# Trunk of two hybrid layers: background dosed by an account of VectorE's backlog, block products chained in PSUM, sums of x in larger pieces

## The chip, the cores and the metric

The kernel runs on one core of a Trainium2 chip. The metric is the device time of one execution in microseconds. The kernel before takes 1490.68 us, the median of three runs (1489.7 to 1491.52). TensorE does the matmuls, VectorE and ScalarE the elementwise work, GpSimd a few masks and the transfers that add into memory, and SyncE issues most other transfers. Each engine runs its own queue of instructions in the order of the program and waits by semaphores for the others.

## The reference

Two layers, each with one projection in, two mixers side by side and one projection out, for a sequence of 256 and a model width of 2048, all in float32:

```python
def hybrid_layer(x, ...):
    u = rms_norm(x, norm_g)
    p = u @ w_in                                  # 2048 x 12304
    qk, v, o, z_a, ig, fg, xb, z_b = jnp.split(p, SPLIT_AT, axis=-1)
    qk = jax.nn.silu(causal_dwconv(qk, qk_conv))
    q, k = jnp.split(qk, 2, axis=-1)
    ...
    h = mlstm_chunkwise(q, k, v, i_pre, log_f)    # 8 heads, matrix memory
    h = h * jax.nn.sigmoid(o)
    h = ((h - mu) * lax.rsqrt(var + EPS)) * head_norm_g
    y_a = h * jax.nn.silu(z_a)
    xc = causal_dwconv(xb, lru_conv_w) + lru_conv_b
    y_b = rg_lru(xc, w_a, b_a, w_x, b_x, lam) * jax.nn.silu(z_b)
    return x + jnp.concatenate([y_a, y_b], axis=-1) @ w_out

def reference(x, ...):
    for l in range(DEPTH):                        # DEPTH = 2
        x = hybrid_layer(x, ...)
    return rms_norm(x, final_g)
```

## The kernel before

**Split products.** Every float32 product is three matmuls in the type float32r: a weight piece W is split into a rounded part `wH` (a cast on ScalarE) and a rest `wL` = W - wH (a subtraction on VectorE), and x likewise. A product is then x_H wH + x_H wL + x_L wH.

**Halves.** The work of TensorE is a list of halves, `order_`. A plain half reads a piece of 128 x 1024 weights and makes 12 matmuls of 512 columns. `prepare` (splits) runs `AHEAD` = 3 halves ahead of the matmuls, and there are four buffers for `wH` and four for `wL`. A raw buffer is loaded by SyncE and becomes free when its second split is done; there are three. After the matmuls of a half, its `after` function evacuates the result if an output is complete.

**Groups.** Each layer has four groups g of two heads. For each group come the projections `o`, `qk`, `v`, `xb`, `z`, `zb`, the gates of the recurrent unit and the products with `w_out` (`out`). Results of `qk`, `xb` and others are in token order and are turned into channels by a transposition on VectorE (`blk`), a store (`moved`) and a load (`fr`).

**Background.** What follows a projection (convolutions `qc` and `xc`, the decay matrix `E`, scores, the scan `xc<-a,gate`, the gating `zb`, `ybH`, `ybL`) is written as generators in a list `bg`. After each plain half `pump` steps through them: a generator does a few instructions and yields what they cost in us of VectorE, or the word "wait", which hands the turn to the next generator. `pump(budget)` grants a fixed amount per half: 1.05 us if at most two main generators are in the list, otherwise 2.6; an overdraft is carried on as a negative credit. `require(key)` steps the generators without regard to the credit until something named is done. `V` and `S` are VectorE and ScalarE behind a proxy that orders each of their background instructions after the last split but one or the last cast that has been written (`LAG`).

**Seven products.** Two projections (`z` of group 2, `o` of group 3) are computed together as a 2 x 2 block product with seven block products instead of eight. A block product is four halves of 6 matmuls (`product`, PSUM tile `ps_b`, lines 1145 to 1147), so 28 short halves are strewn between the plain ones of a layer. They need four sums of blocks of x, S1 to S4, made by `block_sums` on VectorE into two buffers `sums` (S3 and S2 in the first, S1 and S4 in the second), in four pieces of 128 x 256 each with five rows (three additions, a cast, a subtraction). They also need sums of weight blocks, made in memory (`w_d`) by transfers that add, in `weight_sums`. The seven results are combined in `res`, four slots of 128 x 512, by copies and additions after each product, and by three more additions in the background (`end6`).

**The end.** In the last layer the last group's `out` is computed with the second half of its rows in weights that are split into buffers of their own, `w_own`.

## Time and profile before

| | |
|---|---|
| profiled execution, own time | 1490.24 us |
| its span, first to last instruction | 1488.5 us |
| granted TensorE clock | 0.999 |
| TensorE matmuls | 6782 |
| ScalarE busy | 954.8 us, 64% |
| bytes moved from and to memory | 274 GB/s over the span |
| chain that ended last | PE 80%, DVE 8%, DMA 6%, issue 4%, ACT 2% |

In the page PE is TensorE's matmul, PEld its load of the stationary operand, DVE VectorE, ACT ScalarE, POOL GpSimd and SP SyncE. A row of the timeline gives start, duration, engine, line, operation, `out<-in`, shapes, a count, and in brackets how long the engine was idle before it and what ended that. Rows of a group give count, busy time, mean duration in ns and idle time before them. Line L112 is the proxy of `V` and `S`, so nearly all rows of VectorE and ScalarE have it, and names of tiles tell them apart.

Matmuls overlap: each is shown with its whole latency, so TensorE's busy time counts small waits as work. The distance from one start to the next tells more.

### The profile page before, as it was taken

The page shows a single profiled execution, that of the slowest core. Times are in us where ns is not written, and L with a number is a line of the kernel's source. Part 1 is how long each engine was busy: PE and PEld are TensorE (multiplying, and loading weights), DVE is VectorE, ACT ScalarE, POOL GpSimd, SP SyncE. Part 2 cuts the span into 40 slices and gives each one's busy share as a digit, 9 for nine tenths or more (in the row PEclk, how much of TensorE's full clock was granted, in tenths as well). Part 3 has the DMA queues.
Part 4 walks back from the last instruction along what each step waited for, and adds up shares of the span by engine and source line. Part 5 has one row for each costly group of instructions (what it writes and reads, how often), then busy time and mean ns, then how long its engine had stood idle before and what let it go on. Part 6 is the DMA issues. An engine that isn't in the chain of part 4 may idle for free.

```text
span 1488.5 us, 18861 instructions
## 1 busy us (share of the span) xinstructions
PE 1473.6 (99%) x6782; PEld 1226.3 (82%) x6782; DVE 1156.6 (78%) x1648; ACT 954.8 (64%) x1226; POOL 112.2 (8%) x186
## 2 busy tenths in 40 slices
PE   9999999999999999999999999999999999999997
PEld 7888888888888888888788887888888888888886
DVE  5788997687887776778867888977888877767775
ACT  7666766567565765658565567665676567655665
POOL 0020010100100000100000100000001000010002
PEclk9999999999999999999999999999999999999999
DMA  9867898898987988886786667778799668777773
GB/s 331 328 203 245 269 338 268 280 268 268 290 291 249 287 287 265 283 272 234 249 302 198 216 203 235 258 233 264 249 269 322 217 222 247 234 238 263 237 269 123
DMA packets 104046, 383.44 MB, mean 258 GB/s; under 512 B 11392, under 2 KB 31888, under 8 KB 84496
## 3 DMA queue, kind: packets, MB, share of 16 engines
q1 hardware_dynamic: 87536, 327.41, 62.8%
q0 software_dynamic: 13952, 50.35, 15.2%
q10 hardware_dynamic: 2464, 4.47, 0.8%
q8 instruction: 53, 0.87, 0.2%
q14 instruction: 41, 0.34, 0.1%
HBM read 344.95 MB, written 62.41 MB: 274 GB/s over the span
## 4 chain that ended last, share of the span: by engine, by line
PE 80%; DVE 8%; DMA 6%; issue 4%; ACT 2%; SPq 0%; POOL 0%; POOLq 0%; ACTq 0%; DVEq 0%
PE acc L395 67%; DVE wL L112 3%; PE ps_gt L840 2%; DMA x_d<-stage 2%; PE ps_b L1147 1%; PE ps_b L1146 1%; PE ps_b L1145 1%; DMA raw<-in_ws_dram 1%; PE acc L408 1%; DMA rawb<-in_ws_dram 1%; DVE xc L112 1%; DVE gate L112 1%; ACT wH L112 1%; DMA rawb<-w_d 1%; DVE qc L112 1%
## 5 line engine op out<-in xcount | busy, mean ns | idle before, releaser
L395 PE MATMUL acc<-wH,x_s 128*128 128x512 f32 x2752 | 861.0, 390 | 0.4 <-ACT wH L112 0.4
L112 DVE TENSOR_TENSOR wL<-raw,wH 128x1024 fp32r<-128x1024 f32 (+1 forms) x500 | 598.7, 1203 | 222.8 <-ACT wH L112 221.5
L112 ACT CAST wH<-raw 128x1024 fp32r<-128x1024 f32 (+1 forms) x500 | 514.6, 1036 | 359.5 <-PE acc L395 289.8
L395 PEld LDWEIGHTS acc<-wH,x_s 128*128 128x128 f32 x2752 | 516.3, 188 | 107.1 <-ACT wH L112 1.1
L395 PE MATMUL acc<-wL,x_s 128*128 128x512 f32 x1376 | 535.2, 390 | 3.5 <-DVE wL L112 3.5
L395 PEld LDWEIGHTS acc<-wL,x_s 128*128 128x128 f32 x1376 | 258.3, 188 | 59.4 <-DVE wL L112 6.7
L395 PE MATMUL acc<-wH,ybH 128*128 128x512 f32 x224 | 87.2, 390 | 0.3 <-ACT ybH L112 0.3
L395 PE MATMUL acc<-wH,ybL 128*128 128x512 f32 x224 | 87.1, 390 | 0.1
L395 PE MATMUL acc<-wH,yaH 128*128 128x512 f32 x224 | 87.2, 389 | 0.0
L395 PE MATMUL acc<-wL,yaH 128*128 128x512 f32 x224 | 87.2, 389 | 0.0
L395 PE MATMUL acc<-wH,yaL 128*128 128x512 f32 x224 | 87.1, 389 | 0.0
L395 PE MATMUL acc<-wL,ybH 128*128 128x512 f32 x224 | 87.0, 389 | 0.0
L112 ACT ACT_TABLE_LOAD x60 | 77.0, 1283 | 12.1 <-DVE qc L112 6.0
L112 DVE TENSOR_TENSOR wL<-rawb,wH 128x1024 fp32r<-128x1024 f32 x56 | 68.5, 1224 | 13.0 <-ACT wH L112 11.8
L112 ACT CAST wH<-rawb 128x1024 fp32r<-128x1024 f32 x56 | 58.9, 1053 | 26.5 <-PE acc L395 10.0
L516 POOL DMA_DIRECT2D fr<-moved x34 | 19.0, 558 | 546.7 <-DMA moved<-blk 469.2
L395 PEld LDWEIGHTS acc<-wH,ybH 128*128 128x128 f32 x224 | 42.0, 188 | 9.4 <-ACT ybH L112 0.9
L395 PEld LDWEIGHTS acc<-wH,ybL 128*128 128x128 f32 x224 | 42.0, 188 | 9.3 <-DVE ybL L112 0.6
L395 PEld LDWEIGHTS acc<-wH,yaL 128*128 128x128 f32 x224 | 42.0, 188 | 8.8
L395 PEld LDWEIGHTS acc<-wH,yaH 128*128 128x128 f32 x224 | 42.0, 188 | 8.6
L395 PEld LDWEIGHTS acc<-wL,yaH 128*128 128x128 f32 x224 | 42.1, 188 | 8.6
L395 PEld LDWEIGHTS acc<-wL,ybH 128*128 128x128 f32 x224 | 42.0, 188 | 8.6
(218 smaller groups left out, 1627.2 us busy)
## 6 DMA issues: line engine op xcount, KB each, us to landing
raw<-in_ws_dram SPq DMA_DIRECT2D x152, 1024.0 KB, 6.3
raw<-in_ws_dram SPq DMA_DIRECT2D x190, 512.0 KB, 6.0
fr<-moved POOLq DMA_DIRECT2D x34, 512.0 KB, 5.9
moved<-blk SPq DMA_DIRECT2D x132, 128.0 KB, 2.8
w_d<-in_ws_dram POOLq DMA_DIRECT2D x32, 512.0 KB, 9.9
rawb<-w_d SPq DMA_DIRECT2D x32, 512.0 KB, 6.1
rawb<-in_ws_dram SPq DMA_DIRECT2D x24, 512.0 KB, 6.5
x_d<-stage POOLq DMA_DIRECT2D x24, 512.0 KB, 7.7
```

The lines of the kernel that those rows point to most:

```text
L112: ins = f(*a, **k)
L395: st["mm"] = PE.matmul(o, a_[:, kt, P * t : P * t + P], W[:, k], start=b, stop=z)
L408: PE.matmul(ps[:, ct, T * part : 2 * T], W[:, k, P * ct : P * ct + P], moving, start=first and k == 0 and part == 0, stop=last and k == 3 ...
L516: i0 = back.dma_start(out=fr.rearrange("p a c t i -> p a (c t i)"), in_=moved)
L840: PE.matmul(o, W[:, ib, jl], xs[:, ib, a, :], start=j == 0 and i == 0 and W is Hv and a == 0, stop=i == 1 and W is Lv, skip_group_check=True)
L1145: PE.matmul(box["b"], aH, Hv[:, k], start=kp == 0 and k == 0, stop=False)
L1146: PE.matmul(box["b"], aH, Lv[:, k], start=False, stop=False)
L1147: PE.matmul(box["b"], aL, Hv[:, k], start=False, stop=kp == 3 and k == 1)
```

## The change

**The account.** `pump` has no budget. `st["lag"]` estimates VectorE's backlog in us: each step of a generator adds what it yields, splits, transpositions and evacuations add their own costs, and every half takes off 2.72 (a plain half) or 1.36 (a block half), not below zero. Background is given out as long as the account is under `FULL` = 3.6. Some costs are changed: a convolution step 1.45 instead of 1.2, a transposition counted in `swapped`.

**Products.** Their order becomes 1, 2, 5, 3, 6, 7, 4. Product 2 goes on accumulating in PSUM on 1, 3 on 5, and 7 and 4 on 6, and after each the running sum is read. The three additions in the background are gone.

**Sums.** They are made in the order S1, S2, S4, S3. S1 and S2 are made in one piece of 128 x 1024, S4 in two of 512, S3 in four of 256, with a yield after each row except in S3. They begin five waits after the first scan of the layer, and the pieces that overwrite a buffer wait for the product halves that read it, not for whole products.

**Order.** The gates' sigmoids and the `zb` rows of the output by channel are issued on the engines themselves, without the forced order of the proxy. The two sums of weights are made in the other order.

```diff
-    def pump(budget):
-        st["credit"] = min(st["credit"] + budget, budget)
+    def pump():
         i = 0
-        while i < len(bg) and st["credit"] > 0:
+        while i < len(bg) and st["lag"] < FULL:
...
-                st["credit"] -= c
+                st["lag"] += c
...
+            st["lag"] += 1.2          # after prepare(order_[nprep])
...
         if "from" not in hf:
-            pump(1.05 if sum(g not in aside for g in bg) <= 2 else 2.6)
+            pump()
+        st["lag"] = max(0.0, st["lag"] - (1.36 if "from" in hf else 2.72))
...
     def evac_b(l, o, acc):
         require(("rb", l))
-        S.copy(out=o, in_=acc[:, :, 0:T])
-        tt_(o, o, acc[:, :, T : 2 * T], ALU.add)
-        tt_(o, o, bc(st["rb", l], 2), ALU.mult)
-        st["credit"] -= 1.2
+        nc.scalar.copy(out=o, in_=acc[:, :, 0:T])
+        nc.vector.tensor_tensor(out=o, in0=o, in1=acc[:, :, T : 2 * T], op=ALU.add)
+        nc.vector.tensor_tensor(out=o, in0=o, in1=bc(st["rb", l], 2), op=ALU.mult)
+        st["lag"] += 1.2
...
-                    st["sig"] = S.activation(out=o_t[:, ct, :], in_=ps[:, T * j : T * j + T], func=AF.Sigmoid,
-                                             bias=pars[:, l, off : off + 1])
+                    st["sig"] = nc.scalar.activation(out=o_t[:, ct, :], in_=ps[:, T * j : T * j + T], func=AF.Sigmoid,
+                                                     bias=pars[:, l, off : off + 1])
...
-        yield from made(0, "S3", False, x(0, 0), x(1, 0))
+        for _ in range(5):
+            yield "wait"
         yield from made(1, "S1", False, x(1, 1), x(1, 0))
-        while ("done", l, 7) not in st:
-            yield "wait"
         yield from made(0, "S2", True, s(1), x(0, 0))
-        while ("done", l, 5) not in st:
-            yield "wait"
-        yield from made(1, "S4", True, s(0), x(0, 1))
+        yield from made(1, "S4", True, s(0), x(0, 1), 2, 5)
+        yield from made(1, "S3", False, x(0, 0), x(1, 0), 4, 3)
...
         def product(A, no, kp, need, end):
+            opening = kp == 0 and no in (1, 5, 6)
+
             def f(H, L):
-                if kp == 0:
+                if opening:
                     box["b"] = bank("ps_b")
...
-            (2, plain(0, 1), None, lambda: add(0, 1, box["b"]), (1, 0)),
-            (7, summed(0), "S3", lambda: copied(2), 1),
-            (5, summed(1), "S1", lambda: copied(3), 0),
-            (6, summed(0), "S2", end6, 0),
-            (3, summed(1), "S4", lambda: add(1, 1, box["b"]), (1, 1)),
-            (4, plain(1, 1), None, end4, 0),
+            (2, plain(0, 1), None, lambda: copied(0), (1, 0)),
+            (5, summed(1), "S1", lambda: add(3, 1), 0),
+            (3, summed(1), "S4", lambda: add(2, 1), (1, 1)),
+            (6, summed(0), "S2", lambda: add(2, 2), 0),
+            (7, summed(1), "S3", end7, 1),
+            (4, plain(1, 1), None, lambda: add(1, 1), 0),
```

**What stands where now.** First VectorE's queue at the end of group 0 of the first layer, from the scan of `xc` on; `sum_t` and `sums` are rows of a sum of x. Before:

```order
L112 SCALAR_TENSOR_TENSOR xc<-a,gate_1459 128x256 x4
L112 TENSOR_TENSOR sum_t<-x_s 128x256
L112 TENSOR_TENSOR wL<-raw,wH 128x1024
L112 TENSOR_TENSOR sum_t<-sum_t,x_s 128x256
L112 TENSOR_TENSOR zb<-xc,fr 128x1024
L112 TENSOR_TENSOR sum_t<-sum_t,x_s 128x256
L112 TENSOR_TENSOR wL<-raw,wH 128x1024
L112 CAST sums_742<-sum_t 128x256
L112 TENSOR_TENSOR zb<-zb,zsg 128x1024
L112 TENSOR_TENSOR sums_742<-sum_t,sums_742 128x256
L112 TENSOR_TENSOR wL<-rawb,wH 128x1024
```

And at the same place now:

```order
L113 SCALAR_TENSOR_TENSOR xc<-a,gate_1458 128x256
L113 TENSOR_TENSOR wL<-raw,wH 128x1024
L113 SCALAR_TENSOR_TENSOR xc<-a,gate_1458 128x256 x3
L113 TENSOR_TENSOR wL<-raw,wH 128x1024 x2
L113 TENSOR_TENSOR wL<-rawb,wH 128x1024
L113 TENSOR_TENSOR zb<-xc,fr 128x1024
L113 TENSOR_TENSOR zb<-zb,zsg 128x1024
L113 TENSOR_TENSOR wL<-raw,wH 128x1024
L113 TENSOR_TENSOR ybL<-zb,ybH 128x512 x2
```

The rows of the sums are gone from here (the first one comes some fifteen rows later), and the splits have moved up.

Second, VectorE's queue at the end of the first layer, where `zb` is made by channel: from the second addition `zb<-zb,acc` to the gating `zb<-zsg,xc`. Before:

```order
L112 TENSOR_TENSOR zb<-zb,acc 128x512
L112 TENSOR_TENSOR wL<-raw,wH 128x1024
L112 TENSOR_TENSOR zb<-zb,rb 128x512
L112 TENSOR_TENSOR gate_5877<-gate_5877,gate_5842 128x1024
L112 TENSOR_TENSOR wL<-raw,wH 128x1024
L112 SCALAR_TENSOR_TENSOR xc<-a,gate_5877 128x256 x4
L112 TENSOR_TENSOR zsg<-zb,zsg 128x512
L112 TENSOR_TENSOR wL<-raw,wH 128x1024
L112 TENSOR_TENSOR zb<-zsg,xc 128x512
```

And now:

```order
L546 TENSOR_TENSOR zb<-zb,acc 128x512
L113 TENSOR_TENSOR wL<-raw,wH 128x1024
L547 TENSOR_TENSOR zb<-zb,rb 128x512
L113 TENSOR_TENSOR gate_5818<-gate_5818,gate_5783 128x1024
L113 TENSOR_TENSOR wL<-raw,wH 128x1024
L113 SCALAR_TENSOR_TENSOR xc<-a,gate_5818 128x256 x2
L113 TENSOR_TENSOR wL<-raw,wH 128x1024
L113 SCALAR_TENSOR_TENSOR xc<-a,gate_5818 128x256 x2
L943 TENSOR_TENSOR zsg<-zb,zsg 128x512
L113 TENSOR_TENSOR wL<-raw,wH 128x1024
L945 TENSOR_TENSOR zb<-zsg,xc 128x512
```

A fourth split has come in between the scans; between the first addition and this one there are four splits before and now.

Third, VectorE's queue in group 0 of the second layer, from the last rows of `E` to the split behind the transposition (`blk`); `qc` rows are steps of the convolution, and `qsg` is its sigmoid. Before:

```order
L112 TENSOR_SCALAR E<-nb,at_7033 128x128
L112 TENSOR_TENSOR wL<-raw,wH 128x1024
L112 SCALAR_TENSOR_TENSOR qc<-ch,pars,qc 128x255
L112 SCALAR_TENSOR_TENSOR qc<-ch,pars,qc 128x254
L112 TENSOR_TENSOR wL<-raw,wH 128x1024
L112 SCALAR_TENSOR_TENSOR qc<-ch,pars,qc 128x253
L112 SCALAR_TENSOR_TENSOR qc<-ch,pars,qc 128x255
L112 SCALAR_TENSOR_TENSOR qc<-ch,pars,qc 128x254
L112 SCALAR_TENSOR_TENSOR qc<-ch,pars,qc 128x253
L112 TENSOR_TENSOR wL<-raw,wH 128x1024
L112 TENSOR_TENSOR qc<-qc,qsg 128x1024
L112 STREAM_TRANSPOSE blk<-tok 128x1024
```

And now, from the `qc` row that follows `E`:

```order
L113 SCALAR_TENSOR_TENSOR qc<-ch,pars,qc 128x253
L113 TENSOR_TENSOR wL<-raw,wH 128x1024
L113 SCALAR_TENSOR_TENSOR qc<-ch,pars,qc 128x255
L113 SCALAR_TENSOR_TENSOR qc<-ch,pars,qc 128x254
L113 TENSOR_TENSOR wL<-raw,wH 128x1024
L113 SCALAR_TENSOR_TENSOR qc<-ch,pars,qc 128x253
L113 SCALAR_TENSOR_TENSOR qc<-ch,pars,qc 128x255
L113 SCALAR_TENSOR_TENSOR qc<-ch,pars,qc 128x254
L113 TENSOR_TENSOR wL<-raw,wH 128x1024
L113 SCALAR_TENSOR_TENSOR qc<-ch,pars,qc 128x253
L113 TENSOR_TENSOR qc<-qc,qsg 128x1024
L113 STREAM_TRANSPOSE blk<-tok 128x1024
```

Seven `qc` rows instead of six follow `E`, and the last one stands behind the third split, not ahead of it.

More of the change, by code (lines that the diff above doesn't have):

```diff
@@ L1025, in block_sums @@
         sums = st["sums", l] = [act.tile([P, 2, 8, P], F32R, tag=f"xa{i}", name=f"sums{i}") for i in range(2)]
-        x_ = st["x"]
-        def part(r, c, a, k):
-            return x_.bitcast(F32)[:, 8 * c + k : 8 * c + k + 2, a, P * r : P * r + P]
-        def made(i, key, negated, p, q):
-            to = sums[i]
-            for k in (0, 2, 4, 6):
-                ks = slice(k, k + 2)
-                t_ = work.tile([P, 2, P], F32, tag="tok", name="sum_t")
-                (pH, pL), (qH, qL) = ([o(a, k, ks) for a in range(2)] for o in (p, q))
-                i0 = stt(t_, pH, -1.0, qH, ALU.mult, ALU.subtract) if negated else tt_(t_, pH, qH, ALU.subtract)
-                order(i0, st["wL"])
-                tt_(t_, t_, pL, ALU.subtract if negated else ALU.add)
-                tt_(t_, t_, qL, ALU.subtract)
-                V.tensor_copy(out=to[:, 0, ks], in_=t_)
-                tt_(to[:, 1, ks], t_, to.bitcast(F32)[:, 0, ks], ALU.subtract)
-                yield 1.6
-                yield "wait"
-                yield "wait"
+        x_ = st["x"].bitcast(F32)
@@ new lines, in block_sums, with made, difference @@
+        res = st["res", l] = act.tile([P, 4, 512], F32, tag="res", name="res")
+        def made(i, key, negated, p, q, pieces=1, after=None):
+            to, n = sums[i], 8 // pieces
+            for k in range(pieces):
+                ks = slice(n * k, n * k + n)
+                while after and ("done", l, after, (k + 1) * 4 // pieces - 1) not in st:
+                    yield "wait"
+                if pieces < 4:
+                    t_ = res[:, 2 : 2 + 2 // pieces].rearrange("p s (k c) -> p (s k) c", k=4)
+                else:
+                    t_ = work.tile([P, n, P], F32, tag="tok", name="sum_t")
+                (pH, pL), (qH, qL) = ([o(a, ks) for a in range(2)] for o in (p, q))
+                def difference():
+                    i0 = stt(t_, pH, -1.0, qH, ALU.mult, ALU.subtract) if negated else tt_(t_, pH, qH, ALU.subtract)
+                    order(i0, st["wL"])
+                for f in (difference,
+                          lambda: tt_(t_, t_, pL, ALU.subtract if negated else ALU.add),
+                          lambda: tt_(t_, t_, qL, ALU.subtract),
+                          lambda: V.tensor_copy(out=to[:, 0, ks], in_=t_),
+                          lambda: tt_(to[:, 1, ks], t_, to.bitcast(F32)[:, 0, ks], ALU.subtract)):
+                    f()
+                    if pieces == 4:
+                        continue
+                    yield 1.2 / pieces + 0.1
+                    yield "wait"
+                    if pieces == 1:
+                        yield "wait"
+                if pieces == 4:
+                    yield 1.9
+                    yield "wait"
+                    yield "wait"
+                st[key, l, k] = True
@@ L1046, in made @@
             st[key, l] = True
         def x(r, c):
-            return lambda a, k, ks: part(r, c, a, k)
+            return lambda a, ks: x_[:, 8 * c + ks.start : 8 * c + ks.stop, a, P * r : P * r + P]
         def s(i):
-            return lambda a, k, ks: sums[i].bitcast(F32)[:, a, ks]
+            return lambda a, ks: sums[i].bitcast(F32)[:, a, ks]
         while ("lru", l, 0) not in st:
             yield "wait"
-        yield from made(0, "S3", False, x(0, 0), x(1, 0))
+        for _ in range(5):
+            yield "wait"
@@ L1383, in tile_trunk @@
             prepare(order_[nprep])
+            st["lag"] += 1.2
             for key in done:
```

66 lines of the change are left out of this document (30 added, 36 removed).

## The prediction

> **What bounds the kernel now.** I read the page's first part, then TensorE's pitch in the chain of waits, then the waits of its weight loads, then single gaps in the timeline.
>
> ```profile
> span 1488.5 us, 18861 instructions
> PE 1473.6 (99%) x6782; PEld 1226.3 (82%) x6782; DVE 1156.6 (78%) x1648; ACT 954.8 (64%) x1226; POOL 112.2 (8%) x186
> 193.56 8.16 PE acc L395 x36
> PEld acc L395 <- DVE wL L112: 6.7, 8, 1.3
> PEld acc L395 <- ACT wH L112: 1.1, 3, 0.8
> PEld acc L395 <- ACT ybH L112: 0.9, 2, 0.8
> PEld ps_gt L840 <- ACT gate L112: 0.9, 2, 0.7
> PEld acc L395 <- DVE ybL L112: 0.6, 1, 0.6
> ```
>
> TensorE is busy for 99% of the span, and the chain shows what that means: 36 matmuls in 8.16 us, one every 0.227 us, although each lasts 0.39. A half unit of 12 matmuls takes 2.72 us. The number of matmuls does not change, so the change can win only what TensorE waits for. The weight loads' waits (total in us, times, longest) add up to 10.2 us in these five rows, 0.7% of the span. The largest row is the wait for `wL`, VectorE's half of the split of a weight piece. Where do these waits lie?
>
> ```profile
> 183.97 0.50 PE L395 MATMUL acc<-wL,x_s 128*128 128x512 f32 x1 [0.87 <-DVE wL L112]
> 310.84 0.50 PE L395 MATMUL acc<-wL,x_s 128*128 128x512 f32 x1 [0.76 <-DVE wL L112]
> 329.67 0.39 PE L840 MATMUL ps_gt<-xcs,wH 128*128 128x256 f32 x1 [0.34 <-DVE xcs L112]
> 428.69 0.50 PE L395 MATMUL acc<-wL,x_s 128*128 128x512 f32 x1 [0.46 <-DVE wL L112]
> 677.21 0.50 PE L840 MATMUL ps_gt<-xcs,wH 128*128 128x256 f32 x2 [0.37 <-ACT gate L112]
> 712.23 0.50 PE L395 MATMUL acc<-wH,ybH 128*128 128x512 f32 x1 [0.33 <-ACT ybH L112]
> 846.01 0.50 PE L395 MATMUL acc<-wL,x_s 128*128 128x512 f32 x1 [0.67 <-DVE wL L112]
> 920.00 0.50 PE L395 MATMUL acc<-wL,x_s 128*128 128x512 f32 x1 [0.22 <-DVE wL L112]
> 923.80 0.50 PE L395 MATMUL acc<-wL,x_s 128*128 128x512 f32 x1 [0.55 <-DVE wL L112]
> ```
>
> A matmul lasts 0.16 us longer than the pitch, so such a gap costs the idle shown plus 0.16, and 0.11 more because the next matmul lasts 0.50 instead of 0.39: idle + 0.27. The nine gaps cost 4.57 + 9 x 0.27 = 7.0 us.
>
> ```profile
> core 0: us, PE busy (x) PEld busy (x) DVE busy (x) ACT busy (x) POOL busy (x), PEclk, DMA share, GB/s
> 169.00:185.00 16.00, 15.13 (x67) 12.21 (x66) 16.00 (x23) 10.77 (x13) 0.68 (x2) 1.00 0.78 248
> 411.00:430.00 19.00, 18.53 (x81) 14.69 (x80) 18.87 (x24) 14.16 (x19) 0.81 (x1) 1.00 0.85 285
> 681.00:714.00 33.00, 32.54 (x170) 27.40 (x169) 29.67 (x34) 25.79 (x35) 0.67 (x2) 1.00 0.61 219
> 908.00:925.00 17.00, 16.23 (x70) 12.79 (x70) 17.00 (x24) 11.05 (x13) 0.66 (x2) 1.00 0.65 202
> ```
>
> In the stretches ahead of 184, 428 and 924 us VectorE is busy 16.00 of 16.00, 18.87 of 19.00 and 17.00 of 17.00 us, although its mean is 78%. So these are bursts of background queued ahead of a split. The gaps at 712 and 846 end chains; those at 311, 329 and 677 follow late transfers, as shown below.
>
> **The change part by part.** All terms are against the profiled execution's own 1490.24 us (span 1488.5 plus 1.74 around it). The median of the three runs shown, 1490.68, is 0.44 higher and they span 1489.7 to 1491.52.
>
> *Bursts spread: -3.5.* At 184 and 924 the sums of x started right behind the scans of `xc` and stood between four splits; at 428 `zb`, `qc`, `zb` stood in one row ahead of a split. In the new order there is no sum row there, and no more than two rows of the `zb` chain stand between two splits. A half gives VectorE 2.72 us: a split and the next 1.5 us. The four gaps ahead of wL at 183.97, 428.69, 920.00 and 923.80 cost 0.87 + 0.46 + 0.22 + 0.55 + 4 x 0.27 = 3.2, and a smaller one at 425 us about 0.3 (a split 0.17 late there, plus the 0.11). I take all of it; the bounds are 0 and 3.5.
>
> *Less work on VectorE: 0.* Gone are the six sums of results; the sums of x do the same elements in fewer rows.
>
> ```profile
> L112 DVE TENSOR_TENSOR res<-res x6: 692/694/696, 428.5 to 1168.3; 128x512 f32<-128x512 f32 x6
> L112 DVE TENSOR_TENSOR sum_t<-sum_t,x_s 128x256 f32<-128x256 f32 x48 | 20.3, 423 | 0.9
> L112 DVE TENSOR_TENSOR wL<-raw,wH 128x1024 fp32r<-128x1024 f32 (+1 forms) x500 | 598.7, 1203 | 222.8 <-ACT wH L112 221.5
> ```
>
> Six rows of 0.694 are 4.2 us; two more additions from PSUM give back 1.4. A sum row of 256 takes 0.423, so four are 1.69, where one row of 1024 takes 1.20 by the split's row. Four sums of 1024 (S1 and S2, both layers) with four such rows each save about 16 x 0.49 = 7.8 us, those of 512 less. None of it is on the path, since VectorE stands 222.8 us ahead of its splits waiting for ScalarE. It counts only inside bursts, where the first term has it. In exchange one row now stands ahead of a split for 1.2 instead of 0.42 us. I take +0.3 for new small gaps (layer 0, around 205 us, where res and qc rows mix); bounds 0 and 1.2, one such row.
>
> *Chains in PSUM: 0.* The same 28 product halves of 6 matmuls run. Three chains are opened instead of seven, and each product still waits for the row that reads the bank before it; that row (0.59 to 0.68) is hidden by the half that always stands between two products (2.72 us). Without this cover it would cost 0.7 for each of 14 products.
>
> *The chain at 712: +1.1.* `zb` by channel must be gated by the scan before the output product can start.
>
> ```profile
> 690.48 0.69 DVE L112 TENSOR_TENSOR zb<-zb,acc 128x512 f32<-128x512 f32 x1
> 709.71 1.22 DVE L112 TENSOR_TENSOR wL<-raw,wH 128x1024 fp32r<-128x1024 f32 x1
> 710.84 0.68 DVE L112 TENSOR_TENSOR zb<-zsg,xc 128x512 f32<-128x512 f32 x1
> ```
>
> VectorE is without idle from the first addition (690.48) to the gating (710.84), and the addition starts when TensorE's result is there. Before, seven splits stand between these rows; in the new order eight do, the new one between the second and third scan. A split moves what follows it by 710.84 - 709.71 = 1.13. The two edits that free this chain from the forced order don't help, since the row stands where it stands. Bounds 0 and 2.3 (two splits).
>
> *The chain at 846: +1.5.* In layer 1, `qc` is finished, then ScalarE loads a table and makes `qsg`, then VectorE goes on to the next split.
>
> ```profile
> 839.90 1.22 DVE L112 TENSOR_TENSOR wL<-raw,wH 128x1024 fp32r<-128x1024 f32 x1
> 840.06 1.28 ACT L112 ACT_TABLE_LOAD   x1 [2.09 <-DVE qc L112]
> 841.35 1.06 ACT L112 ACTIVATE qsg<-qc 128x1024 f32<-128x1024 f32 x1
> 842.45 1.22 DVE L112 TENSOR_TENSOR qc<-qc,qsg 128x1024 f32<-128x1024 f32 x1 [1.33 <-ACT qsg L112]
> ```
>
> Before, a split (839.90) fills part of ScalarE's 2.4 us, and VectorE idles only 1.33. Now the last `qc` row stands behind that split, so the split no longer lies inside the wait: 1.13, and one more `qc` row (0.48) stands behind the same `E`, which waits for a transfer. That is 1.6; I take 1.5, bounds 0 (the transfer comes earlier) and 1.6.
>
> *Late transfers: -1.2.*
>
> ```profile
> 294.78 12.71 DMA x_d<-stage
> x_d<-stage POOLq DMA_DIRECT2D x24, 512.0 KB, 7.7
> 307.57 1.01 ACT L112 COPY stage<-acc 128x1024 f32<-128x1024 f32 x1 [4.58 <-DMA x_d<-stage]
> 671.86 1.05 ACT L112 CAST wH<-raw 128x1024 fp32r<-128x1024 f32 x1 [3.80 <-DMA raw<-in_ws_dram]
> ```
>
> At 311 ScalarE waited 4.58 us to reuse `stage`, since one store took 12.71 us (median 7.7); at 677 a weight load was 3.80 late. 311, 329 and 677 cost 0.76 + 0.34 + 0.37 + 3 x 0.27 = 2.3. The new order of products leaves a product between the two uses of the rewritten weight sum, and the gate's sigmoids need no longer follow a cast. But the same bytes move. I take half, 1.2; bounds 0 and 2.3. The Trainium skill ("Trainium Kernel Development and Optimization", Key Constraints) says that transfers of all issuing engines run on the same 16 DMA engines and interleave; by it a store slowed by neighbours is only moved, and the sum would be 1.2 higher. The 12.71 against 7.7 agrees with it.
>
> *The end: +0.8.*
>
> ```profile
> 1455.50 0.33 SPq L331 DMA_DIRECT2D raw<-in_ws_dram  x1
> 1457.30 1.29 DVE L112 TENSOR_TENSOR ybL<-zb,ybH 128x512 fp32r<-128x512 f32 x2 [0.69 <-ACT ybH L112]
> 1461.83 2.00 ACT L112 CAST wH<-raw 128x1024 fp32r<-128x1024 f32 x2 [0.24 <-DMA raw<-in_ws_dram]
> 1466.42 0.39 PE L1240 MATMUL acc_x<-wL,ybH 128*128 128x512 f32 x1
> ```
>
> The last weight load waits until the second split into `w_own` has freed its buffer. Before, that split stands between the two `zb` rows, and the load is issued at 1455.50. Now all four stand behind `ybL`. By the rows: the two `zb` rows end 1.1 earlier, then ybH and ybL (2.0), then cast and two splits (some 2.6), so the issue comes at about 1458.5, 3 us later. The data took 6.2 us (to 1461.73), then a cast 1.05 and a split 1.2: 1467.2, where TensorE wants `wL` at 1466.42. That is 0.8; bounds 0 and 3.1 (the loads just ahead took up to 8.5).
>
> Sum: -3.5 + 0.3 + 1.1 + 1.5 - 1.2 + 0.8 = -1.0, so 1490.24 - 1.0 = 1489.2.
>
> **Rivals.** *Faster: the account also clears the chains.* If the layer runs with less lag, the ends at 712, 846 and 1466 have slack: -3.5 - 1.2 = -4.7, 1485.5; with all transfers -5.8, 1484.4. For it: none of these rows is in TensorE's own order. Against: the chains start from TensorE's results, so they gain no lead.
> *Transfers only move:* 1489.2 + 1.2 = 1490.4.
> *The change doesn't do what it says:* the account counts VectorE's work, but 311, 677 and 846 wait for ScalarE or a transfer. Then bursts return elsewhere, and half of the first term goes: 1489.2 + 1.8 = 1491.0.
> *Slower: the last load.* If it lands 8.5 us after its issue, the end costs 3.1 instead of 0.8; it decides from about 5.5 us on. With transfers only moved and the small gaps at 1.2 the sum is -3.5 + 1.2 + 1.1 + 1.5 + 3.1 = +3.4: 1493.6.
>
> **How the numbers follow.** About 0.2% (3 us) is what a measurement of this kernel can tell from no change: below 1487.7 is faster, above 1493.7 slower. The forecast, 1489.2, and what lies within a microsecond and a half of it has 0.42; transfers only moved or bursts that return, 0.18; the faster rival 0.29; the slower one 0.11. The forecast's own range is 1487.7 to 1490.8. So faster 0.29, same 0.60, slower 0.11. For 8 in 10 the range leaves out the far half of the faster rival and most of the slower one: 1485.6 to 1492.6.
>
> **What would show it.** Bursts: no TensorE gap at 184, 428, 920 and 924, and VectorE's share below 1 there. The chain at 712: `ybH` releases TensorE with about 1.5 us of idle instead of 0.33. The chain at 846: an idle of about 2 us ahead of `wL`. The end: a gap ahead of `acc_x<-wL,ybH`. Transfers: no wait of `stage`. I am wrong if gaps appear inside the block products (`ps_b` waiting for `sums`), or if the weight loads' waits don't fall although the bursts are gone.

## The result: 0.33% slower, and where the profile shows it

The changed kernel takes 1494.67 us, the median of ten runs (1489.45 to 1497.66), against 1489.75 for the kernel before, measured beside it ten times. The ratio is 1.0033 with a 95% interval of 1.0023 to 1.0044. The prediction was 1489.2 with a range of 1485.6 to 1492.6, so it was wrong in direction and range. The profiled execution of the changed kernel took 1497.22 us, 6.98 more than that of before; it is one of the slower of its ten.

First the page's first part for the changed kernel, then the waits of TensorE's weight loads (total in us, times, longest):

```profile
span 1495.5 us, 18788 instructions
PE 1475.5 (99%) x6782; PEld 1229.5 (82%) x6782; DVE 1142.9 (76%) x1564; ACT 956.3 (64%) x1226; POOL 106.2 (7%) x186
```

```profile
PEld acc L395 <- ACT wH L113: 3.9, 3, 1.6
PEld acc L395 <- DVE wL L113: 2.9, 3, 1.3
PEld ps_gt L843 <- ACT gate L848: 2.8, 1, 2.8
PEld acc L395 <- ACT ybH L113: 2.1, 1, 2.1
PEld ps_S L722 <- DVE Pt L113: 1.8, 1, 1.8
```

VectorE did become 14 us lighter, and the wait for `wL`, 6.7 us before, is 2.9. But fewer and much longer waits have come in its place. The timeline of TensorE shows where they lie:

```profile
209.09 0.50 PE L395 MATMUL acc<-wL,x_s 128*128 128x512 f32 x1 [0.57 <-DVE wL L113]
334.87 0.55 PE L843 MATMUL ps_gt<-xcs,wH 128*128 128x256 f32 x2 [2.51 <-ACT gate L848]
621.39 0.39 PE L722 MATMUL ps_S<-qks 128*128 128x256 f32 x1 [1.47 <-DVE Pt L113]
716.31 0.50 PE L395 MATMUL acc<-wH,ybH 128*128 128x512 f32 x1 [1.70 <-ACT ybH L113]
851.63 0.50 PE L395 MATMUL acc<-wH,x_s 128*128 128x512 f32 x1 [1.22 <-ACT wH L113]
853.08 0.50 PE L395 MATMUL acc<-wL,x_s 128*128 128x512 f32 x1 [0.95 <-DVE wL L113]
```

With 0.27 us added to each as in the prediction, these six cost 8.42 + 1.62 = 10.0 us, where the nine of before cost 7.0. The gaps at 184, 311, 329, 428, 677, 920 and 924 are gone. That is 3 us more, and the profiled execution lost 7. The rest stands in the windows view, cut here at the places where the granted clock changes:

```profile
core 0: us, PE busy (x) PEld busy (x) DVE busy (x) ACT busy (x) POOL busy (x), PEclk, DMA share, GB/s
331.78:335.19 3.41, 0.90 (x6) 0.58 (x6) 2.94 (x6) 3.40 (x8) 0.00 (x0) 1.00 0.31 119
335.19:338.61 3.42, 3.42 (x15) 3.16 (x14) 3.39 (x5) 3.03 (x7) 0.00 (x0) 0.50 0.64 180
338.61:342.02 3.41, 3.41 (x16) 2.79 (x15) 0.67 (x2) 3.40 (x6) 0.00 (x0) 1.00 0.91 274
714.08:717.49 3.41, 1.71 (x7) 0.78 (x5) 2.94 (x4) 2.10 (x3) 0.00 (x0) 1.00 0.55 233
717.49:720.90 3.41, 3.28 (x9) 2.57 (x9) 2.10 (x4) 0.62 (x1) 0.00 (x0) 0.50 0.79 279
850.61:854.02 3.41, 1.44 (x5) 1.00 (x6) 3.41 (x4) 3.41 (x5) 0.00 (x0) 1.00 0.35 69
854.02:857.43 3.41, 3.41 (x10) 2.66 (x9) 3.41 (x4) 1.38 (x3) 0.50 (x1) 0.50 1.01 282
```

Behind three of the waits the granted clock is 0.50 for exactly 3.41 us, and then 1.00 again. In the second and third of these windows TensorE starts 8 matmuls instead of the 15 of 0.227 us each that would fill it (the x9 and x10 of the view count those still running from before too). By start-to-start distances the three cost some 1.55 us each, 4.7 together. The kernel before has no such window in its profiled execution between its first 7 us and its last 4. The three begin at 335.19, 717.49 and 854.02; the distances, 382.30 and 136.53, are 112 and 40 times 3.413. So in this execution the windows lie on a fixed grid; whether that holds in the other runs too is answered at the end.

### The profile page after: what moved, and what is told of

It is laid out like the page before. It is cut to its first block, busy times and chain, and to the rows that moved or that the text cites. A ratio compares the mean times of both kernels' runs of the same rounds, so it can differ in the third digit from the quotient of the medians.

```text
span 1495.5 us, 18788 instructions
## 1 busy us (share of the span) xinstructions
PE 1475.5 (99%) x6782; PEld 1229.5 (82%) x6782; DVE 1142.9 (76%) x1564; ACT 956.3 (64%) x1226; POOL 106.2 (7%) x186
## 4 chain that ended last, share of the span: by engine, by line
PE 84%; DVE 5%; DMA 5%; issue 3%; ACT 2%; SPq 0%; POOL 0%; ACTq 0%; POOLq 0%; DVEq 0%
PE acc L395 71%; DMA raw<-in_ws_dram 4%; PE ps_gt L843 3%; DVE wL L113 3%; PE ps_b L1154 1%; PE ps_b L1155 1%; PE ps_b L1153 1%; PE acc L408 1%; DVE qc L113 1%; ACT wH L113 1%; ACT L113 1%; PE acc L1251 1%; PE acc L1252 1%; PE acc L1250 1%; DMA fr<-moved 0%
## 5 line engine op out<-in xcount | busy, mean ns | idle before, releaser
L113 DVE STREAM_TRANSPOSE blk<-tok 128x1024 f32<-128x1024 f32 x33 | 41.0, 1241 | 16.0 <-ACT tok L113 12.6
```

Source lines behind the costliest of these rows:

```text
L113: ins = f(*a, **k)
```

## Experiments

Words used below: the **account** is the new `pump` with `st["lag"]` and the yields that go with it; the **products** are the new order of products, PSUM chains, sums of x and order of the two weight sums; the **freed rows** are the gates' sigmoids and the `zb` rows by channel without the forced order. "At 848" means the place of the chain predicted for 846, which moves by a few us between kernels.

### First: the parts apart, a larger FULL, and a ladder of stalls

The account alone, on the kernel before (the same `pump`, `lag` and yields as in the change, nothing else):

```diff
-    def pump(budget):
-        st["credit"] = min(st["credit"] + budget, budget)
+    def pump():
...
-                st["credit"] -= c
+                st["lag"] += c
...
-            pump(1.05 if sum(g not in aside for g in bg) <= 2 else 2.6)
+            pump()
+        st["lag"] = max(0.0, st["lag"] - (1.36 if "from" in hf else 2.72))
```

> The kernel before with the account alone: products, sums of x, forced order and the order of the weight sums are as before. Theory A (the account lengthens the chains, and every TensorE stall of about 2 us or more is followed by some 3 us at half clock): TensorE stalls of over 1 us near 712 and near 848 us as in the changed kernel, a stretch of half clock behind each, and 1493 to 1497 us. Rival B (the new products, sums and their order did it, through transfers that come late and results that are read late): no stall over 1 us at these places, and 1489 to 1491 us.

Measured: 1489.14 us (1486.41 to 1491.5, 11 runs), ratio 0.9989 (0.998 to 0.9999). The account alone lengthens the chain at 848 just as in the change, but at 712 it doesn't, and the time is slightly better. A wait of 1.47 us stands at 722 instead, where the kernel before has none. Theory A fell as the whole story: it expected 1493 to 1497.

The products and freed rows with the fixed grants, that is the change with the lines above turned round:

> The changed kernel with the fixed grants and the yields of before; products, sums, the freed rows and the order of the weight sums are the new ones. Theory A: the stall near 848 is back at the 0.9 us of before, the one at 712 at 1 us or less (one split fewer stands in the chain), no stretch of half clock, and the bursts at 184 and 924 stay away because the sums no longer stand there: 1486 to 1489 us. Rival B: the waits at 335 (gate) and 621 (scores) that the changed kernel showed are still there, and 1492 to 1496 us.

Measured: 1487.65 us (1486.14 to 1492.83, 11 runs), ratio 0.9984 (0.9974 to 0.9995). Rival B, with its waits at 335 and 621, fell too. Neither part alone loses anything; **together they lose 0.33%**. TensorE's timeline of this kernel at the two chains:

```profile
710.91 0.50 PE L395 MATMUL acc<-wH,ybL 128*128 128x512 f32 x1 [0.66 <-DVE ybL L112]
843.98 0.50 PE L395 MATMUL acc<-wL,x_s 128*128 128x512 f32 x1 [0.95 <-DVE wL L112]
```

The waits of 1.70 and 1.22 + 0.95 in the change are 0.66 and 0.95 here. It had been expected that the bursts stay away, but a wait of 1.00 us for `wL` stands at 919, and a new one of 1.18 at 1068.

The change with a larger limit:

```diff
-FULL = 3.6
+FULL = 6.0
```

> The changed kernel with FULL = 6.0 instead of 3.6, so that background is given out earlier. Theory A: the convolution of group 0 of layer 1 is done before the decay matrix waits for its transfer, so the stall near 848 falls under 0.5 us; the chain at 712 loses one or two of its splits and keeps 0 to 1 us; the price is deeper queues ahead of the splits, so gaps of 0.5 to 1 us in bursts return: 1488 to 1492 us. Rival C (any account at all is worse, since what counts is the number of rows ahead of a split): 1495 us or more.

Measured: 1502.88 us (6 runs), ratio 1.0071 (1.0052 to 1.009): rival C. Two waits at 411 and 415 us alone are 2.83 and 3.36 in its timeline, both for splits that stand behind background. The wait at 848 didn't shrink either.

The ladder of stalls, on the kernel before: a small matmul reads `ones` at the start of a half, GpSimd fills `ones` again with the same value several times, and a second one at the start of the next half waits for that. The result of these matmuls is not used.

```diff
+            k_ = stops.get(st["n"])
+            if k_ is not None:
+                if k_:
+                    st["stop"] = psum.tile([P, 2, 512], F32, tag="acc0" if st["pair"] else "acc1", name="stop")
+                PE.matmul(st["stop"][:, 0, 0:P], ones, ones, start=True, stop=True)
+                for _ in range(k_):
+                    G.memset(ones.bitcast(F32), 1.0)
```

> The kernel before with 15 added stops of TensorE: a small matmul that reads a tile which GpSimd has filled again 14 to 29 times (0.2 us each) since the last half began, so TensorE stands still for some 0.5 to 3.5 us. Theory A: stalls up to about 1.6 us are followed by matmuls at 0.227 us pitch, stalls from about 1.9 us on by some 3 us at twice that pitch, so the longer ones cost 1.2 to 1.6 us more than they last. Rival D (the half clock of the changed kernel has nothing to do with its stalls): the pitch behind every stall is 0.227 us and the granted clock is 0.999 as in the kernel before.

Measured in a single run, 1520.27 us. Most stops were shorter than meant, and one waited 11.5 us behind another transfer in GpSimd's queue. Two of them in the timeline, and the windows around them:

```profile
331.48 0.33 PE L390 MATMUL stop<-ones 128*128 128x128 f32 x1 [1.48 <-POOL ones L392]
...
1167.86 0.33 PE L390 MATMUL stop<-ones 128*128 128x128 f32 x1 [2.01 <-POOL ones L392]
```

```profile
328.97:332.38 3.41, 1.93 (x9) 1.32 (x8) 3.15 (x6) 2.21 (x4) 2.00 (x9) 1.00 0.84 296
332.38:335.80 3.42, 3.42 (x26) 3.19 (x25) 2.43 (x5) 3.22 (x4) 0.00 (x0) 1.00 0.87 280
1165.18:1168.59 3.41, 1.40 (x7) 0.85 (x7) 2.36 (x2) 1.92 (x3) 2.05 (x10) 1.00 1.02 422
1168.60:1172.00 3.40, 3.40 (x10) 2.62 (x9) 1.66 (x2) 1.46 (x2) 0.00 (x0) 0.51 0.93 337
```

The wait of 1.48 us is followed by full clock, that of 2.01 by a window at half. Of the other stops, the one of 11.5 us was followed by half clock and those of 0.24 to 1.37 us were not. Nothing but the stop was done to TensorE there, so rival D falls: the half clock is made by the stall.

### Second: which pair of parts, and chains mended

The change without the freed rows (`S` and `tt_` again, yields 0.6 again):

```diff
...
-                    st["sig"] = nc.scalar.activation(out=o_t[:, ct, :], in_=ps[:, T * j : T * j + T], func=AF.Sigmoid,
+                    st["sig"] = S.activation(out=o_t[:, ct, :], in_=ps[:, T * j : T * j + T], func=AF.Sigmoid,
...
-            nc.vector.tensor_tensor(out=zb[:, sl_, :], in0=sg, in1=xc[:, sl_, :], op=ALU.mult)
-            yield 0.2
...
+            tt_(zb[:, sl_, :], sg, xc[:, sl_, :], ALU.mult)
+            yield 0.6
```

> The changed kernel with the freed rows put back under the forced order (evacuation by channel, gating by channel, gate sigmoids); the account and the new products and sums stay. Theory A2 (the loss is the chain at 712, which the account and the freed rows lengthen together by one split, plus the chain near 848, plus a window of half clock wherever over 2.1 us of idle fall into one window of the clock's grid): the stall at 712 falls from 1.9 us to 0.6 or less and no half clock follows there, the one near 848 stays at 2.5 us: 1490 to 1492 us. Rival E (account and new products together make transfers late, seen at 335 and 621): these two stalls stay, and 1493 to 1496 us.

Measured: 1493.24 us (6 runs), ratio 1.0026 (1.0015 to 1.0038). Its timeline:

```profile
333.73 0.55 PE L843 MATMUL ps_gt<-xcs,wH 128*128 128x256 f32 x2 [2.53 <-ACT gate L113]
...
713.64 0.50 PE L395 MATMUL acc<-wH,ybH 128*128 128x512 f32 x1 [0.39 <-ACT ybH L113]
726.73 0.47 PE L395 MATMUL acc<-wH,yaH 128*128 128x512 f32 x1 [1.47 <-DVE x_acc L113]
```

The gate's wait at 334 stays although its sigmoids follow the casts again: rival E. The wait at 712 shrinks, but one of 1.47 at 727 comes for it, so the freed rows only moved some 1.4 us from 727 to 712.

The account and the freed rows without the products:

> The kernel before with the account and the freed rows; products, sums and the order of the weight sums are as before. Theory A2: a stall of 1.6 to 2.1 us at 712 and of 2.5 us near 848, half clock behind one or both of them in many runs: 1491 to 1495 us. Rival E: without the new products no late transfer at 335 and 621, and about 1489 us as with the account alone.

Measured: 1489.19 us, ratio 1.0003 (0.9993 to 1.0012). The wait at 712 is 1.70 as in the change, with half clock behind it and behind 848 in the profiled run, but there is no wait at 335, and no loss in the median. Theory A2, which expected 1491 to 1495, fell as the whole story. So what loses is **the account with the products**.

Both chains mended in the changed kernel (freed rows ordered again, and fewer rows behind `E`):

```diff
-                yield 1.45
+                yield 1.45 if g or not l else 0.7
```

> The changed kernel with both chains mended: the freed rows under the forced order as in the run with account and products, and in group 0 of layer 1 a convolution step yields 0.7 instead of 1.45, so that five qc rows and two splits stand between the decay matrix and the gating of qc instead of seven rows and three splits. Theory A2: at most 0.6 us at 712, at most 0.5 us near 848, no half clock at these places: 1486.5 to 1489.5 us. Rival E: the waits at 335 and 621 keep it at 1491 us or more.

Measured: 1493.18 us, ratio 1.0028 (1.002 to 1.0037). The chain at 848 did give way (0.29 and 0.92 us, where 0.5 or less had been expected). At 712 the wait is 0.39, but with it came the one of 1.47 at 727, as in the run with account and products: what is gone there is the half clock behind the wait, more than the wait. The time fell by only 1.5 us. By start-to-start distances the gate's wait at 333 was 2.4 us again. Rival E.

The changed kernel again, without any edit:

> The changed kernel once more, to see which of its stalls come back. Theory A2: 1493 to 1496 us; about 1.9 us at 712 and 2.5 us near 848 again, since they are chains of instructions; the half clock behind them depends on where the clock's windows fall and can be gone or at other places; 335 and 621 come back smaller or not at all, since they follow late transfers. Rival E: 335 and 621 come back in the same size.

Measured: 1494.79 us (6 runs), ratio 1.0044 (1.0031 to 1.0056). All waits came back, 335 too, with 3.3 us from start to start. So it is no accident of one run; its cause is in the program.

### Third: the transfers behind the wait at 335

In the changed kernel, GpSimd's queue and ScalarE's around the wait, and transfers issued from 300 to 330 us with their median time to landing:

```profile
304.79 0.87 POOL L987 DMA_DIRECT2D x_d<-stage  x1 [10.51 <-ACT stage L113]
305.34 2.85 POOL L1096 DMA_DIRECT2D w_d<-in_ws_dram  x3
343.15 0.58 POOL L517 DMA_DIRECT2D fr<-moved  x1 [34.96 <-DMA moved<-blk]
```

```profile
322.52 1.05 ACT L113 CAST wH<-raw 128x1024 fp32r<-128x1024 f32 x1 [0.92 <-PE acc L395]
329.51 1.05 ACT L113 CAST wH<-raw 128x1024 fp32r<-128x1024 f32 x1 [5.94 <-DMA raw<-in_ws_dram]
```

```profile
raw<-in_ws_dram SPq DMA_DIRECT2D x6, 512.0 KB, 9.9
...
w_d<-in_ws_dram POOLq DMA_DIRECT2D x3, 512.0 KB, 18.6
```

Three adding transfers of the weight sums stand between the store `x_d<-stage` and the load `fr<-moved`. They have nothing of their own to wait for, so GpSimd issues all three the moment the store's own wait ends, at 305.3 us. They land after 18.6 us (median), the raw loads beside them after 9.9, where the kernel before has 6.7 between 300 and 330 us. A cast comes 5.94 us late, ScalarE then has a table load, two rows of `sz` and a cast ahead of the gate's sigmoids, and TensorE waits for these. In the kernel before and with the account alone, one such transfer follows the store; with the products and the fixed grants, two. Over all the profiled kernels but the one with stops, the median landing of the 512 KB raw loads from 300 to 330 us rises with the number of adding transfers behind the store: 4.7 us with none, 4.9 to 6.7 with one, 6.0 to 6.8 with two, 8.1 to 10.5 with three. `weight_sums` counts turns of `pump` ("wait" yields), and which turns it gets depends on the account and on the order of products: that is why neither part does it alone.

```diff
+GAP = 6
...
+                while st["n"] < st.get("n_w", -99) + GAP:
+                    yield "wait"
+                st["n_w"] = st["n"]
                 order(G.dma_start(out=wd[l][to][j][:, cs], in_=src, accum_op=ALU.add), st["gq"])
```

> The changed kernel, with at least six halves between two adding transfers of the weight sums, so that one of them instead of three stands in GpSimd's queue between the store x_d<-stage at 305 us and the next load fr<-moved. Theory F (the account and the new order of products together put three adding transfers behind that store; GpSimd issues them within 3 us, they slow the raw loads, and the cast that comes 6 us late ends in the gate's stall at 335 and its window of half clock): the raw loads around 320 land in 6 to 7 us instead of 9.9, the stall at 335 falls from 2.4 to 3.3 us to under 0.7, its half clock goes, and the time falls by 3 to 4.5 us to 1490 to 1492 us. Rival G (the stall comes from ScalarE's queue, where the gate's sigmoids stand behind sz and two casts): it stays over 2 us, and so does 1494 to 1495 us.

Measured: 1491.6 us, ratio 1.0005 (0.9994 to 1.0017). One transfer follows the store, the raw loads land in 5.6 us and the wait at 335 is gone. But the spacing is in halves of the program, not in time, and elsewhere three met again behind another waiting transfer:

```profile
391.63 0.55 POOL L518 DMA_DIRECT2D fr<-moved  x1 [19.46 <-DMA moved<-blk]
392.17 2.56 POOL L1100 DMA_DIRECT2D w_d<-in_ws_dram  x3
```

```profile
415.34 0.49 PE L396 MATMUL acc<-wH,x_s 128*128 128x512 f32 x1 [1.22 <-ACT wH L114]
416.60 0.71 PE L396 MATMUL acc<-wL,x_s 128*128 128x512 f32 x1 [0.77 <-DVE wL L114]
```

The opposite, on the kernel with fixed grants and products:

```diff
+                for _ in range(3 if (l, no) == (0, 5) else 0):
+                    yield "wait"
                 for j, h in parts:
```

> The kernel of the run with the old grants, with three more waiting turns ahead of the third pass of the weight sums in layer 0, and nothing else: three adding transfers instead of two stand behind the store at 304 us. Theory F: the stall at 331 to 335 us grows from 1.2 us (0.76 + 0.45) to 2.4 us or more, with half clock behind it where over 2.1 us fall into one window of the clock: 1489 to 1492 us against 1487.65. Rival G: no such stall, within 0.5 us of 1487.65.

Measured: 1490.92 us, ratio 1.0002 (0.9991 to 1.0014), where it was 0.9984. Three transfers follow the store instead of two, and the waits from 325 to 331 us grow from 1.2 to 2.2. The profiled run also shows one of 3.2 at 405 to 408 that comes from a late `fr`; whether the edit made that one is open, and so is how much of the loss of 3.3 us belongs to the three transfers.

All three places mended (six halves between transfers, freed rows ordered, 0.7 per step):

> The changed kernel with the adding transfers six halves apart and both chains mended as in the earlier run (freed rows ordered again, 0.7 instead of 1.45 per convolution step in group 0 of layer 1). Theory F with A2: no stall over 2 us anywhere but the one of 1.6 us at 727 and of 1.6 us at 620, no window of half clock behind the start: 1488 to 1490 us, so the account with all its bad places mended about equals the kernel before and is not better than the old grants with the new products (1487.65). Rival G: 1492 us or more.

Measured: 1490.13 us, ratio 0.9995 (0.9985 to 1.0004), no window of half clock behind the start in the profiled run. The loss is gone.

Then only two transfers held back, and the same with mended chains:

```diff
-                    while ("loaded", l, no, 2 * j + h) not in st:
+                    while ("loaded", l, no, 2 * j + h) not in st or (l, no, j) == (0, 5, 1) and st["n"] < 120:
```

> The changed kernel with nothing moved but two adding transfers of weight sums in layer 0: they are written behind the load fr<-moved instead of ahead of it, so one or two instead of three follow the store at 305 us, and (unlike the run with six halves between them) no other place gets three. Theory F: the stall at 335 is under 0.7 us, none appears at 415, and 1490 to 1491.5 us remain (the chains at 712 and near 848 are untouched). Rival G2 (spacing helped there only because it moved later products' transfers too): the stall at 335 stays over 2 us, 1494 us or more.

> The same two transfers held back, and both chains mended (freed rows ordered again, 0.7 instead of 1.45 per convolution step in group 0 of layer 1). Theory F with A2: no window of half clock behind the start, the largest stalls 1.6 us at 727 and 1.6 us at 620: 1487.5 to 1489.5 us. Rival G2: 1491 us or more.

Measured: 1493.22 us, ratio 1.0024 (1.0014 to 1.0035), and 1492.05 us, ratio 1.0013 (1.0004 to 1.0022). GpSimd's queue and the raw loads in the first of them:

```profile
303.92 0.87 POOL L987 DMA_DIRECT2D x_d<-stage  x1 [10.51 <-ACT stage L113]
304.47 1.19 POOL L1096 DMA_DIRECT2D w_d<-in_ws_dram  x1
```

```profile
raw<-in_ws_dram SPq DMA_DIRECT2D x6, 512.0 KB, 6.2
```

The wait at 335 is gone in both profiled runs, as theory F has it. But both times were missed: the medians fell by only 1.5 and 1.1 us against the change and the mended chains, where F had 3 to 4.5 for this wait, and 1492.05 lies where rival G2 had it. The 1.5 itself is uncertain: drawing the runs anew at random puts it between -1.5 and 4.4, so F's figure isn't excluded. The place is explained, its size in the median is not: the two kernels still scatter from 1488 to 1497 and from 1489 to 1494, and the profiled run is one of many.

The granted clock explains a part of the first. Its profiled run, 1489.43 us, had a mean clock of 0.999; the twelve runs go from 0.999 (1488.46 to 1491.37 us) down to 0.994 (1495.83 and 1497.37). Their mean is 0.9971, that of the kernel before beside them 0.9986, and (0.9986 - 0.9971) x 1490 = 2.2 us of the 3.5 lost, by that estimate. The chains at 712 and 848 were left as they were in this kernel. With mended chains the mean is 0.9982, which by the same estimate is some 0.6 of the 2.4 lost; the rest is open.

Hence the price of all adding transfers, left out from the changed kernel, from the kernel before, and from the change with mended chains. The output is another one there (weight sums without the added terms), all other instructions stay in the program.

```diff
-            else:
-                order(G.dma_start(out=wd[l][to][j][:, cs], in_=src, accum_op=ALU.add), st["gq"])
```

> The changed kernel without the 32 adding transfers of the weight sums (four of the seven block products then use weights that are not summed, so the output is another one); every instruction of the other engines stands where it stood. Theory H (about half of the loss comes from how the adding transfers meet the raw loads, not from the chains): no late raw load at 329, no stall at 335, 1488.5 to 1490.5 us, so at most 2.5 us above the kernel before without these transfers. Rival A3 (the chains at 712 and near 848 with their windows of half clock are the loss, and the transfers only shift it about): still 4 to 5 us above the kernel before without them.

> The kernel before without the same 32 adding transfers (again another output). Theory H: it gains less than the changed kernel does from the same cut: 0.5 to 2 us, 1487.5 to 1489 us, since in it the adding transfers mostly come one by one. Rival A3: both gain the same.

> The changed kernel with both chains mended, without the 32 adding transfers (another output). Theory H with A2: neither cause is left, 1486.5 to 1488.5 us, at or below the kernel before without them. Rival A3: the same, but with the change itself 4 to 5 us higher. If it stays over 1490 us, the account costs something else that neither theory names.

Measured: 1488.85, 1486.22 and 1487.51 us (11 runs each; before beside them 1489.72), ratios 0.999 (0.9982 to 0.9999), 0.9977 (0.9968 to 0.9986) and 0.9983 (0.9974 to 0.9992). So the same transfers cost the change 1494.67 - 1488.85 = 5.8 us and the kernel before 3.5, more than the 0.5 to 2 expected. Of the loss of 4.9 us, **2.3 come from how the adding transfers meet the others, and 2.6 remain without them**, of which mended chains take back 1.3. These are differences of medians, and drawing the runs anew at random puts the 2.3 between 0.3 and 5.0 and the 2.6 between 1.1 and 3.5. The 2.6 lies just over the 2.5 of theory H and well under the 4 to 5 of rival A3. In the change without the transfers neither 335 nor 621 is left as a wait. Here the chains stand alone, first the change, then before:

```profile
710.40 0.50 PE L395 MATMUL acc<-wH,ybH 128*128 128x512 f32 x1 [1.70 <-ACT ybH L113]
843.84 0.51 PE L395 MATMUL acc<-wH,x_s 128*128 128x512 f32 x1 [0.84 <-ACT wH L113]
845.30 0.50 PE L395 MATMUL acc<-wL,x_s 128*128 128x512 f32 x1 [0.95 <-DVE wL L113]
```

```profile
707.95 0.50 PE L395 MATMUL acc<-wH,ybH 128*128 128x512 f32 x1 [0.34 <-ACT ybH L112]
842.01 0.50 PE L395 MATMUL acc<-wL,x_s 128*128 128x512 f32 x1 [0.96 <-DVE wL L112]
```

They are 1.4 and 1.1 us (0.84 + 0.27) longer, in kernels without adding transfers. Behind 845 the first of them has a window of half clock, the other two kernels have none. The mean clocks of the three are 0.9975, 0.9984 and 0.9983, so by the estimate above the clock is 1.3 us of the 2.6, about what mended chains take back. The other 1.3, in which even the mended kernel lies above the one before, has no cause shown.

### A kernel that beats both

Fixed grants, products and freed rows, with the convolution of group 0 of layer 1 given out earlier:

```diff
-                yield 1.2
+                yield 1.2 if g or not l else 0.5
```

> The kernel with the old grants and the new products, and in group 0 of layer 1 a convolution step yields 0.5 instead of 1.2: two splits instead of three stand between the decay matrix and the gating of qc, and the last five qc rows lie ahead. Theory A2 (the chain near 848 is set by the rows and splits in it): the stall of 1.6 us there falls under 0.5 and the time by about 1 us, to 1486 to 1488 us, faster than the kernel before by 0.15 to 0.25%. Rival (the transfer that the decay matrix waits for sets it): the stall stays at 1 us or more, and 1487.5 to 1489 us.

Measured: 1487.96 us (1486.42 to 1490.1, 11 runs), ratio 0.9984 (0.9975 to 0.9992). The wait at 848 is gone, as expected, and the time did not fall below that of the same kernel without the edit (1487.65): a new wait has come behind it, for the results of the same group.

```profile
864.36 0.35 PE L658 MATMUL ps_n<-vH,PH 128*128 128x258 f32 x1 [2.03 <-DVE hh L112]
```

Both kernels are 0.16% faster than the one before and some 0.5% faster than the change. What helped in the change are the products and freed rows with the fixed grants (which of the two wasn't separated); what hurt is the account on top of the products.

## Why the prediction was wrong, step by step

**Bursts, -3.5: right.** None of the gaps at 184, 428, 920 and 924 is left. In the stretches ahead of them VectorE is busy 14.91 of 16.00, 16.91 of 19.00 and 16.78 of 17.00 us; in the last it is nearly as full as before, so there the order of the rows, not a lighter stretch, must have taken the gap away.

**New small gaps, +0.3; PSUM chains, 0; VectorE's lighter work, 0: right in kind.** One gap came, at 209 us, for 0.57 + 0.27 = 0.84, inside the bounds. No product waited for a sum or a bank.

**The chain at 712, +1.1: right, and mis-sized a little.** It went from 0.60 to 1.97, +1.4. VectorE's rows in the changed kernel show the predicted split between the scans:

```profile
709.41 1.27 DVE L113 TENSOR_TENSOR_SCAN xc<-a,gate 128x256 f32<-128x256 f32 x2
710.59 1.21 DVE L113 TENSOR_TENSOR wL<-raw,wH 128x1024 fp32r<-128x1024 f32 x1
711.71 1.28 DVE L113 TENSOR_TENSOR_SCAN xc<-a,gate 128x256 f32<-128x256 f32 x2
```

The prediction said that freeing the rows did not help here. That is so, and with the account ordered rows do better at this place: with them no split stands between `zsg` and `zb`, as one does before and in the change, and the wait is 0.39. But 727 pays for it.

**The chain at 848, +1.5: right, and mis-sized.** From 0.94 it went to 1.22 + 0.95 + 2 x 0.27 = 2.71, +1.8, just over the bound of 1.6. VectorE in the changed kernel:

```profile
845.45 1.22 DVE L113 TENSOR_TENSOR wL<-raw,wH 128x1024 fp32r<-128x1024 f32 x1
846.58 0.48 DVE L113 SCALAR_TENSOR_TENSOR qc<-ch,pars,qc 128x253 f32<-128x253 f32 x1
849.52 1.23 DVE L113 TENSOR_TENSOR qc<-qc,qsg 128x1024 f32<-128x1024 f32 x1 [2.47 <-ACT qsg L113]
```

As foreseen, the last `qc` row stands behind the split, and VectorE then idles the whole 2.47 us of ScalarE's table load and sigmoid, where it idled 1.33.

**Late transfers, -1.2: the first step that failed.** The waits at 311, 329 and 677 went, 2.3 us as the best case had it. But 335 (2.51 + 0.27) and 621 (1.47 + 0.27) came, 4.5 us, so the term is +2.2 in the profiled run. The prediction bounded it by 0 and 2.3 of gain because the same bytes move, and asked only whether late transfers stay. It never asked who gives the adding transfers their turns. `weight_sums` is paced by turns of `pump`, and the change rewrote `pump` and the order of products that its last pass follows. The cause of 335 is shown by spacing and holding back; of 621 only the late load ahead of it was seen, and that it is gone without the adding transfers. The Trainium skill ("Trainium Kernel Development and Optimization", Key Constraints) says that transfers from all the issuing queues share 16 DMA engines and interleave, which the prediction took to mean that transfers are only moved. The bytes were, but three together cost more than one at a time: the raw loads beside three landed in 8.1 to 10.5 us, beside one in 4.9 to 6.7.

**The end, +0.8: not seen.** No wait of `acc_x` shows in the changed kernel. The last load was issued at 1463.79 and TensorE asked for its `wL` at 1473.89, 10.1 us later; before, it was 1455.50 and 1466.42, so 10.9. The load lost 0.8 us against TensorE where the prediction had 3, and its cast began 4.9 us after the issue, where it had been 6.2. The prediction's own terms, 1458.5 + 6.2 + 1.05 + 1.2, also make 1467.0 and not 1467.2.

**The clock: missing from the sum, the second step that failed.** The prediction put the cost of a longer wait at idle + 0.27 and nothing for what follows it. Three windows of half clock came, 4.7 us in the profiled execution and the largest term of all. By the grid a wait can be free of it or not: in the change it came behind 712 and 848, with the account alone the same 1.11 + 0.96 us at 848 fell into two windows, and nothing followed. That is a good part of the scatter (8.2 us in the change, 3.9 before): of the ten runs of the change, the one at 0.998 took 1489.45 us, the four at 0.994 to 0.996 took 1494.77 to 1497.66. The mean granted clock is 0.9964 over the 16 runs of the change and 0.9982 over 132 of the kernel before; estimated from that, the clock took (0.9982 - 0.9964) x 1490 = 2.7 us of the mean loss. It overlaps with the parts above, since the waits make it.

The terms of the profiled execution, -3.5 + 0.8 + 1.4 + 1.8 + 2.2 + 0 + 4.7 = 7.4, stand against 6.98 measured. Without the two failed steps, the forecast's own terms would have given +0.5: no change, which is where the prediction stood.

**Open:** why the kernel with two transfers held back and mended chains still loses 2.4 us, of which the clock is some 0.6; and what the 1.3 us are by which the change with mended chains and without adding transfers still lies above the kernel before without them.

## What to carry to other kernels

Two edits that are each harmless can meet in a third thing: here a side task paced by turns of the scheduler. Ask of every rewritten scheduler which work is paced by its turns, transfers above all, and pace transfers by what they must follow, so that they can't gather behind one waiting entry of a queue. Spread waits rather than gather them: by the prices below, four gaps of half a us that lie apart cost two, and one wait of 2.1 us within a window of the clock costs 2.1 and some 1.6 of half clock behind it.

## What the runs showed of the hardware

**The clock's grid.** In all 19 profiled executions the granted clock changed only at multiples of 3.413 us from one another; where the grid lies against the first instruction differs from one to the next. Sum TensorE's standstill (start-to-start distance less the pitch) within each full-clock cell of this grid: every cell with 2.10 us or more was followed by a cell at clock 0.50, none with 2.08 or less was. The two nearest are the change without adding transfers at 843 us (2.10, half clock next) and the kernel with FULL = 6.0 at 407 us (2.08, full clock). A half-clock cell cost 1.4 to 1.7 us. The Trainium skill ("TensorE: Matmul & The Clock Gate", Part 1, What's actually happening) describes a free-running window of about 3.4 us and half clock after an idle one; window and half clock agree with the 3.413 and 0.50 here. Its rule in the same part (HAM oscillation), to avoid idle gaps over about 3.4 us, is too mild by these runs: 2.1 us within one window are enough, in one gap or in two.

**GpSimd's queue gathers transfers.** An entry that waits (a store for ScalarE's copy, a load for another transfer) holds those behind it, and then all leave at once: three within 2.85 us behind the store at 305 in the change, three within 2.56 behind the load at 392 with the sums spaced.
